# Peer layer, dense stage: its loads asked for in a fixed order four halves ahead, its gated rows sent from ScalarE's queue, its weight tables and maxima in small parts

## The chip, the core and the metric

The kernel runs on one core of a Trainium2 chip. The metric is the device time of one execution in microseconds (us). Each engine runs its own stream of instructions in the order in which the program holds them: TensorE (PE, with its weight loads as PEld), VectorE (DVE), ScalarE (ACT), GpSimd (POOL) and SyncE (SP). Transfers run on 16 DMA engines; SP, ACT and POOL ask for them, and an instruction that has to wait for something holds up whatever stands behind it in its stream.

## The reference

One transformer layer over 512 tokens of width 2048: an adaptive norm, a mixer (attention beside a recurrent unit), and a layer of 16,384 experts. Only the last matters here:

```
q = (h @ w_q) ...                       # two score vectors of 128 keys for each of 8 heads
v1, i1 = top_k(s1, 16); v2, i2 = top_k(s2, 16)
vs, ic = top_k(v1[..., :, None] + v2[..., None, :], 16)   # 16 of the 256 sums
e = i1[ic // 16] * 128 + i2[ic % 16]    # expert numbers: 128 per token
w = softmax(vs)
act = gelu(u[e] . h) * w                # 128 dot products per token
y = sum over the 128 of act * v[e]
```

`peer_u` and `peer_v` are 16,384 x 2048 in float32, 128 MB each.

## The kernel before, in words

Three of the four token groups of 128 (their numbers are 0, 2 and 3) are computed densely: all of `peer_u` is read once and multiplied with these 384 tokens. The fourth group, called side work here, fetches its 128 rows per token straight from `peer_u` and `peer_v`.

The dense stage runs over 128 blocks of 128 experts (`ublock`, L685), and each block over two halves of 1024 elements, so 256 halves. A half reads 512 KB into one of four `raw` buffers (`stream`, whose load is L99 on SP), rounds it on ACT into `shi` (L94), takes the rest on DVE into `slo` (L95), and PE multiplies: 8 pieces x 3 products (`shi` with `dh`, `shi` with `dl`, `slo` with `dh`), 24 matmuls of 384 columns (L690). `shi` and `slo` have three buffers each. After both halves ACT applies the gelu (L694) and SP writes the gated rows `ge` to two tables in HBM, 128 KB (L696) and 64 KB (L698).

`pump()` stands after every half. It sends on the side work at a rate of 0.9 (`side.send(GRATE)`): POOL asks for 128 rows, 1 MB, by an indirect DMA (L744) into one of four `gr` buffers, and two gathers later DVE uses it, for the dot products (L758, 128 times) or for the sum `y` (L756, 128 times). It also sends on one `scatter` (L886) when some are due.

Beside that, three more things run within the 128 blocks:

- `decode` (L624, L627, L628, operations on 128x2048 elements): from the top sixteen sums to expert numbers, once per token group. Group 0's stands before the first block, those of groups 2 and 3 before blocks 2 and 3, and the late group's after its own top-k (`tp0`, L588 to L604), whose scores SP reads back head by head (`s12`, L934, two buffers).
- `halves_of`: the weights of the chosen experts as a dense matrix. For each half-batch of 64 tokens 16 groups of four tokens: DVE makes one-hot tiles (L909, L914), PE multiplies them (L915), ACT copies the result into `ws` (L916). When the half-batch is done, SP writes `ws` to the tables in four parts of 1 MB (L920), in 256-byte pieces, and DVE takes four maxima `F` (L921). There are six half-batches.
- `make_list`: from the maxima to lists of the experts in use (L822, L823), with scatters on POOL.

A `pad` tile is set to zero on DVE (L811) and written to the first rows of the tables, and a `padi` to the lists (L812, L813, L817). It lies in memory that the decodes of groups 2 and 3 used before.

A scheduler simulates the engines and reorders each engine's stream by its own estimates. An instruction under `keep_in_program_order` stays behind the one that was written before it on its engine; only the gathers, the scatters and one step of the lists are so marked before.

After the dense stage the v stage (from about 2356 us) gathers the rows of `peer_v` that are in use, with their gates from the tables, and multiplies them; the rest of the side work's `y` runs beside it.

Of the kernel before, what the change touches and what calls it, by code (L numbers as in the profile page):

```python
# [9 lines left out]
F32 = mybir.dt.float32  # L10
F32R = mybir.dt.float32r
# [4 lines left out]
OP = mybir.AluOpType  # L16
AX = mybir.AxisListType
# [7 lines left out]
NB = 128  # L25
# [34 lines left out]
def program(ctx: ExitStack, tc: tile.TileContext, a):  # L60
    nc = tc.nc
    V, A, PE, G = nc.vector, nc.scalar, nc.tensor, nc.gpsimd
# [5 lines left out]
    raw = pool(ctx, "raw", 4)  # L68
    hl = pool(ctx, "hl", 3)
# [23 lines left out]
    def hilo(hi, lo, src):  # L93
        A.copy(hi, src)  # L94
        V.tensor_tensor(out=lo, in0=src, in1=hi, op=OP.subtract)  # L95

    def stream(src, n=1024):
        r = raw.tile([128, 1024], F32, name="raw")
        nc.sync.dma_start(r[:, :n], src)  # L99
        hi = hl.tile([128, 1024], F32R, name="shi")  # L100
        lo = hl.tile([128, 1024], F32R, name="slo")
        hilo(hi[:, :n], lo[:, :n], r[:, :n])
        return hi, lo
# [14 lines left out]
    tab1 = dram.tile([NROW + 128, 256], F32, name="tab1")  # L118
    tab2 = dram.tile([NROW + 128, 512], F32, name="tab2")
# [16 lines left out]
    for half in range(2):  # L136
        r = raw.tile([128, 1024], F32, name="raw")[:1]
# [31 lines left out]
    def pbank():  # L169
        return ps.tile([128, 512], F32, name="pj", tag="pj", bufs=2)  # L170

    for q in range(4):
        p = pbank()
# [7 lines left out]
    with tc.tile_pool(name="pro", bufs=1, reuse_waits="tile") as pro:  # L181
# [7 lines left out]
        for t in range(NT):  # L189
# [7 lines left out]
            r = rstd(pro, ss, 1, 1.0 / D)  # L197
            dg = pro.tile([128, 128], F32, name="dg", bufs=2)
            V.tensor_scalar(dg, ident, r, None, op0=OP.mult)
            for k4 in range(4):  # L200
                p = pbank()
# [62 lines left out]
    p = pbank()  # L264
# [9 lines left out]
    p = bank()  # L274
# [211 lines left out]
    for b0 in range(0, 8, 2):  # L486
# [6 lines left out]
        ge = [lru_y(b) for b in bs]  # L493
# [26 lines left out]
    for q in range(4):  # L520
# [8 lines left out]
        for k2 in range(KC // 2):  # L529
            w = stream(a["w_out"][q, k2])  # L530
# [8 lines left out]
        for t in range(NT):  # L539
# [4 lines left out]
            m = mp.tile([128, 512], F32, name="x1", tag="m")  # L544
# [5 lines left out]
            if q == 3:  # L550
                s4 = const.tile([128, 1], F32, name="s4", bufs=4)
                V.tensor_reduce(s4, ssq[:, t], axis=AX.X, op=OP.add)
                w = const.tile([128, 128], F32, name="dg", bufs=4)
# [6 lines left out]
    with tc.tile_pool(name="wk2", bufs=12, reuse_waits="tile") as wk2:  # L560
        for q in range(4):
            pr = bank()
            for k4 in range(4):
                k = q * 4 + k4
                p = bank()
# [80 lines left out]
    for h in range(H):  # L646
# [6 lines left out]
        for half in range(2):  # L653
            p = pbank()
# [10 lines left out]
            p = bank()  # L665
            c0 = half * 128
# [13 lines left out]
            G.tensor_copy(dl[k], wl2[k][:, 128:])  # L680
    hps.close()

    def ublock(b):
        p = pbank()
        for half in range(2):  # L685
            uh, ul = stream(a["peer_u"][b, half])
            for k8 in range(8):
                k = half * 8 + k8
                for i, (l, r) in enumerate(three(uh, ul, dh[k], dl[k])):
                    PE.matmul(p[:, :NDT], l[:, k8 * 128:k8 * 128 + 128], r, start=(k == 0 and i == 0),  # L690
                              stop=(k == KC - 1 and i == 2))
            pump()
        ge = gq.tile([128, NDT], F32, name="ge")
        A.activation(ge, p[:, :NDT], AF.Gelu_apprx_tanh)  # L694
        rows = slice(128 + b * 128, 256 + b * 128)
        nc.sync.dma_start(tab2[rows].rearrange("p (t x) -> p t x", t=2)[:, :, 0:128],  # L696
                          ge[:, 128:384].rearrange("p (t x) -> p t x", t=2))
        nc.sync.dma_start(tab1[rows, 0:128], ge[:, 0:128])  # L698

    dn = ExitStack()  # L700
    otp = pool(dn, "otp", side="right")
# [3 lines left out]
    todo = []  # L705
# [5 lines left out]
    def ublocks(upto):  # L711
        while blk[0] < upto:
            ublock(blk[0])
            blk[0] += 1
# [76 lines left out]
    def scatter_some(n):  # L791
        for _ in range(n):
            if scatters:
                scatters.pop(0)()

    todo.append(lambda: side.send(GRATE))
    todo.append(lambda: scatter_some(1))
    for t in (1, 2):
# [97 lines left out]
    TH = 64  # L896
    sets = {}

    def halves_of(dz, t, o, tab, c0, lo, step):
        Fs = []  # L900
        for hf in range(2):
            h0 = hf * TH
            ws = dz.tile([128, NB, TH], F32, name="ws")
            for t4 in range(TH // 4):
                ublocks(lo + hf * step + t4 * (step - 3) // (TH // 4))
                p = bank()
                o1 = dz.tile([128, 4, 128], F32, name="o1", bufs=2)
                t0 = h0 + t4 * 4
                V.tensor_tensor(out=o1, in0=iota[:, None, :].to_broadcast([128, 4, 128]),  # L909
                                in1=o[:, 0, t0:t0 + 4, None].to_broadcast([128, 4, 128]), op=OP.is_equal)  # L910
                for j in range(4):
                    tt = t0 + j
                    o2 = dz.tile([128, 128], F32, name="o2", bufs=6)
                    V.tensor_scalar(o2, iota, o[:, 1, tt:tt + 1], o[:, 2, tt:tt + 1], op0=OP.is_equal, op1=OP.mult)  # L914
                    PE.matmul(p[:, j * 128:j * 128 + 128], o2, o1[:, j], start=True, stop=True)  # L915
                A.copy(ws[:, :, t4 * 4:t4 * 4 + 4].rearrange("p i t -> p t i"), p.rearrange("p (t i) -> p t i", t=4))  # L916
            F = dz.tile([128, NB], F32, name="F", bufs=4)
            for i in range(4):
                sl = slice(i * 32, i * 32 + 32)
                nc.sync.dma_start(tab[128 + i * 4096:4224 + i * 4096, c0 + h0:c0 + h0 + TH].rearrange("(i p) t -> p i t", p=128), ws[:, sl])  # L920
                V.tensor_reduce(F[:, sl], ws[:, sl], axis=AX.X, op=OP.max)  # L921
            Fs.append(F)
        V.tensor_tensor(out=Fs[0], in0=Fs[0], in1=Fs[1], op=OP.max)
        return Fs[0]
# [191 lines left out]
    r = inv(1)  # L1116
# [75 lines left out]
```

## Time and profile before

| | us |
|---|---|
| median of 3 runs | 3125.18 (3118.3 to 3130.12) |
| the profiled execution | 3117.84 |
| its span | 3116.0 |
| dense stage (first L690 to the last) | about 1073 to 2356 |
| v stage and end | 2356 to 3116 |

The columns of the profile: a group of instructions is given by line, engine, operation and tiles with its count, its busy time, the mean of one in ns, and the idle time of the engine just ahead of it with what ended that. Over the whole span PE is busy 92%, DVE 80%, ACT 39% and POOL 30%, and the 16 DMA engines move 279 GB/s.

### The profile page before, as it was taken

The page shows a single profiled execution, that of the slowest core. Times are in us where ns is not written, and L with a number is a line of the kernel's source. Part 1 is how long each engine was busy: PE and PEld are TensorE (multiplying, and loading weights), DVE is VectorE, ACT ScalarE, POOL GpSimd, SP SyncE. Part 2 cuts the span into 40 slices and gives each one's busy share as a digit, 9 for nine tenths or more (in the row PEclk, how much of TensorE's full clock was granted, in tenths as well). Part 3 has the DMA queues.
Part 4 walks back from the last instruction along what each step waited for, and adds up shares of the span by engine and source line. Part 5 has one row for each costly group of instructions (what it writes and reads, how often), then busy time and mean ns, then how long its engine had stood idle before and what let it go on. Part 6 is the DMA issues. An engine that isn't in the chain of part 4 may idle for free.

```text
span 3116.0 us, 39002 instructions
## 1 busy us (share of the span) xinstructions
PE 2859.3 (92%) x14093; PEld 2497.1 (80%) x14093; DVE 2487.7 (80%) x4100; ACT 1221.3 (39%) x1653; POOL 928.6 (30%) x673
## 2 busy tenths in 40 slices
PE   7899999989999999988899989998878999888887
PEld 5577777768788899988889989998877777766665
DVE  6877777873368898999988889999768888777777
ACT  5322223662232243333322223334223444555665
POOL 0000000000020002222223352422448777477774
PEclk9999999999999999999999999999989999999999
DMA  9767777333322368999999989999989999978885
GB/s 344 292 226 232 246 234 237 111 106 129 122 89 90 109 203 331 334 320 304 313 394 402 400 307 345 347 297 307 343 336 397 371 353 359 350 278 321 344 317 218
DMA packets 329502, 869.30 MB, mean 279 GB/s; under 512 B 125682, under 2 KB 181362, under 8 KB 274388
## 3 DMA queue, kind: packets, MB, share of 16 engines
q0 software_dynamic: 72512, 477.03, 40.5%
q1 hardware_dynamic: 256352, 389.52, 37.3%
q8 instruction: 112, 1.84, 0.2%
q14 instruction: 90, 0.74, 0.1%
q10 hardware_dynamic: 436, 0.18, 0.0%
HBM read 805.38 MB, written 61.25 MB: 278 GB/s over the span
## 4 chain that ended last, share of the span: by engine, by line
PE 56%; DVE 12%; DMA 10%; issue 7%; ACT 3%; POOL 2%; SPq 1%; another core or an unknown queue 0%; DVEq 0%; ACTq 0%; POOLq 0%
PE pj L690 25%; PE ps L991 11%; PE pj L660 6%; PE ps L526 4%; DMA araw<-w_ada 4%; DVE slo L95 4%; PE pj L302 3%; PE pj L991 2%; PE ps L915 2%; DVE gr L758 1%; DMA raw<-tab,igown 1%; PE pj L526 1%; DVE F L921 1%; ACT shi L94 1%; POOL gr L744 1%
## 5 line engine op out<-in xcount | busy, mean ns | idle before, releaser
L690 PE MATMUL pj<-dh,slo 128*128 128x384 f32 x2048 | 698.9, 343 | 53.7 <-DVE slo L95 53.5
L690 PE MATMUL pj<-dh,shi 128*128 128x384 f32 x2048 | 699.6, 342 | 21.1 <-ACT shi L94 21.1
L690 PE MATMUL pj<-dl,shi 128*128 128x384 f32 x2048 | 696.8, 340 | 0.0
L94 ACT CAST shi<-raw 128x1024 fp32r<-128x1024 f32 (+1 forms) x402 | 417.6, 1047 | 632.8 <-PE pj L690 243.5
L95 DVE TENSOR_TENSOR slo<-raw,shi 128x1024 fp32r<-128x1024 f32 (+1 forms) x402 | 487.7, 1217 | 217.1 <-ACT shi L94 196.3
L690 PEld LDWEIGHTS pj<-dh,slo 128*128 128x128 f32 x2048 | 392.4, 192 | 60.8 <-DVE slo L95 60.4
L95 DVE TENSOR_TENSOR slo<-gr,shi 128x1024 fp32r<-128x1024 f32 x342 | 405.6, 1222 | 41.4 <-ACT shi L94 34.6
L690 PEld LDWEIGHTS pj<-dh,shi 128*128 128x128 f32 x2048 | 393.3, 192 | 22.2 <-ACT shi L94 22.2
L690 PEld LDWEIGHTS pj<-dl,shi 128*128 128x128 f32 x2048 | 392.5, 192 | 0.1
L94 ACT CAST shi<-gr 128x1024 fp32r<-128x1024 f32 x342 | 342.1, 1046 | 107.6 <-PE ps L991 60.2
L744 POOL DMA_INDIRECT gr<-u_rows,ei x128 | 173.9, 1358 | 678.5 <-DVE gr L758 313.9
L756 DVE SCALAR_TENSOR_TENSOR y<-gr,dots,y 128x2048 f32<-128x2048 f32 x128 | 300.7, 2349 | 36.7 <-DMA gr<-v_rows,ei 36.4
L991 PE MATMUL ps<-shi,gh 128*128 128x512 f32 x740 | 254.0, 414 | 73.3 <-ACT gh L94 42.0
L148 DVE SCALAR_TENSOR_TENSOR araw<-araw,sil 128x1024 f32<-128x1024 f32 x192 | 233.8, 1222 | 104.8 <-DMA araw<-w_ada 101.9
L991 PE MATMUL ps<-slo,gh 128*128 128x512 f32 x740 | 297.4, 408 | 6.9 <-DVE slo L95 6.9
L758 DVE SCALAR_TENSOR_TENSOR gr<-gr,hrow 128x2048 f32<-128x2048 f32 x128 | 292.3, 2284 | 4.0 <-issue 4.0
L744 POOL DMA_INDIRECT gr<-v_rows,ei x128 | 198.3, 1549 | 311.4 <-DVE y L756 161.3
L991 PE MATMUL ps<-shi,gl 128*128 128x512 f32 x740 | 275.2, 399 | 1.6 <-DVE gl L95 1.6
L679 POOL CAST dh<-hh 128x384 fp32r<-128x384 f32 x16 | 10.4, 648 | 855.1 <-DVE hh L573 855.1
L991 PEld LDWEIGHTS ps<-shi,gh 128*128 128x128 f32 x740 | 143.9, 196 | 122.2 <-ACT gh L94 50.3
L694 ACT ACTIVATE ge<-pj 128x384 f32<-128x384 f32 x128 | 62.8, 490 | 422.4 <-PE pj L690 334.5
L302 PE MATMUL pj<-hh,shi 128*128 128x512 f32 x528 | 214.0, 405 | 6.6 <-ACT w L478 3.5
(353 smaller groups left out, 4996.2 us busy)
## 6 DMA issues: line engine op xcount, KB each, us to landing
raw<-peer_u SPq DMA_DIRECT2D x256, 512.0 KB
araw<-w_ada SPq DMA_DIRECT2D x192, 512.0 KB
raw<-w_in SPq DMA_DIRECT2D x66, 512.0 KB
tab<-ws SPq DMA_DIRECT2D x24, 1024.0 KB
raw<-w_out SPq DMA_DIRECT2D x32, 512.0 KB
raw<-w_q SPq DMA_DIRECT2D x32, 512.0 KB
tab<-ge SPq DMA_DIRECT2D x128, 128.0 KB
tab<-ge SPq DMA_DIRECT2D x128, 64.0 KB
```

What stands on the lines that cost most here:

```text
L94: A.copy(hi, src)
L95: V.tensor_tensor(out=lo, in0=src, in1=hi, op=OP.subtract)
L148: V.scalar_tensor_tensor(out=r, in0=r, scalar=1.0, in1=sil[:, half * 1024:half * 1024 + 1024], op0=OP.mult, op1=OP.mult, accum_out=acc[:, ...
L302: PE.matmul(p, l[:, k8 * 128:k8 * 128 + 128], r, start=(k == 0 and i == 0), stop=(k == KC - 1 and i == 2))
L526: PE.matmul(po[t], l[:, ts], r[:, sl], start=(k == 0 and i == 0), stop=(k == KC - 1 and i == 2))
L660: PE.matmul(p, l[:, k8 * 128:k8 * 128 + 128], r, start=(k == 0 and i == 0), stop=(k == KC - 1 and i == 2))
L690: PE.matmul(p[:, :NDT], l[:, k8 * 128:k8 * 128 + 128], r, start=(k == 0 and i == 0), stop=(k == KC - 1 and i == 2))
L694: A.activation(ge, p[:, :NDT], AF.Gelu_apprx_tanh)
L744: return G.indirect_dma_start(out=out, out_offset=None, in_=src, in_offset=bass.IndirectOffsetOnAxis(ap=idx, axis=0))
L756: V.scalar_tensor_tensor(out=y0, in0=r, scalar=dots[:, j:j + 1], in1=y0, op0=OP.mult, op1=OP.add)
L758: V.scalar_tensor_tensor(out=r, in0=r, scalar=1.0, in1=hrow, op0=OP.mult, op1=OP.mult, accum_out=dots[:, j:j + 1])
L991: PE.matmul(banks[t][half * 2 + q2], l[:, ts], x[:, sl], start=first and i == 0, stop=end and i == 2)
```

## The change

Loads. The `peer_u` loads have a function of their own (`uload`). Before each half it asks for loads up to four halves ahead, and each load is kept in program order on SP: it stays behind the SP instruction that was written just before it, whichever that is.

Gated rows. The two `ge` writes of a block leave from ACT's queue.

Weights and maxima. A half-batch writes `ws` in 32 parts of 128 KB, each kept in program order on SP, and its four maxima stand between them as single entries of a list; `pump()` takes five entries of that list after every half. The token groups of a half-batch end two blocks sooner, and the blocks that are left of its share run after them.

```diff
+    loads = []
+    asked = [0]
+
+    def uload(upto):
+        while asked[0] < min(upto, 2 * NB):
+            r = raw.tile([128, 1024], F32, name="raw")
+            tc.keep_in_program_order(nc.sync.dma_start(r, a["peer_u"][asked[0] // 2, asked[0] % 2]))
+            loads.append(r)
+            asked[0] += 1
+
     def ublock(b):
         p = pbank()
         for half in range(2):
-            uh, ul = stream(a["peer_u"][b, half])
+            uload(2 * b + half + 4)
+            uh = hl.tile([128, 1024], F32R, name="shi")
+            ul = hl.tile([128, 1024], F32R, name="slo")
+            hilo(uh, ul, loads.pop(0))
...
-        nc.sync.dma_start(tab2[rows].rearrange("p (t x) -> p t x", t=2)[:, :, 0:128],
+        nc.scalar.dma_start(tab2[rows].rearrange("p (t x) -> p t x", t=2)[:, :, 0:128],
                           ge[:, 128:384].rearrange("p (t x) -> p t x", t=2))
-        nc.sync.dma_start(tab1[rows, 0:128], ge[:, 0:128])
+        nc.scalar.dma_start(tab1[rows, 0:128], ge[:, 0:128])
...
+    slices = []
+
+    def slices_some(n):
+        for _ in range(n):
+            if slices:
+                slices.pop(0)()
+
+    todo.append(lambda: slices_some(5))
     todo.append(lambda: side.send(GRATE))
     todo.append(lambda: scatter_some(1))
...
-                ublocks(lo + hf * step + t4 * (step - 3) // (TH // 4))
+                ublocks(lo + hf * step + t4 * (step - 5) // (TH // 4))
...
-            for i in range(4):
-                sl = slice(i * 32, i * 32 + 32)
-                nc.sync.dma_start(tab[128 + i * 4096:4224 + i * 4096, c0 + h0:c0 + h0 + TH].rearrange("(i p) t -> p i t", p=128), ws[:, sl])
-                V.tensor_reduce(F[:, sl], ws[:, sl], axis=AX.X, op=OP.max)
+
+            def write(i, ws=ws, c=c0 + h0):
+                tc.keep_in_program_order(nc.sync.dma_start(
+                    tab[128 + i * 512:640 + i * 512, c:c + TH].rearrange("(i p) t -> p i t", p=128), ws[:, i * 4:i * 4 + 4]))
+
+            def most(i, ws=ws, F=F):
+                V.tensor_reduce(F[:, i * 32:i * 32 + 32], ws[:, i * 32:i * 32 + 32], axis=AX.X, op=OP.max)
+
+            for i in range(32):
+                slices.append(lambda i=i, w=write: w(i))
+                if i % 8 == 4:
+                    slices.append(lambda i=i // 8, m=most: m(i))
+            ublocks(lo + hf * step + step)
             Fs.append(F)
```

Three places show how the streams differ. In the changed kernel the load is L689, the gather use for the dots L771, the one for `y` L769, the pad writes L833, L834 and L838, the one-hot tiles L930 and L935, the `s12` loads L964, the `ws` writes L941.

SP before, where the writes of `pad` and `padi` stand: 33 loads of `peer_u` have been asked for by then.

```order
L99 DMA raw<-peer_u 128x1024 x2
L696 DMA tab_87<-ge 256x1x128
L698 DMA tab_86<-ge 128x128
L99 DMA raw<-peer_u 128x1024
L812 DMA tab_87<-pad 128x512
L813 DMA tab_86<-pad 128x256
L817 DMA list_88<-padi 128x16
```

SP of the changed kernel at the same place; the first row is the load of the side group's token rows `hrow`:

```order
L735 DMA hrow<-hspill 128x2048
L689 DMA raw<-peer_u 128x1024 x4
L673 DMA sspill<-sc_8295 128x128
L689 DMA raw<-peer_u 128x1024 x5
L833 DMA tab_87<-pad 128x512
L834 DMA tab_86<-pad 128x256
L838 DMA list_88<-padi 128x16
L838 DMA list_89<-padi 128x20
L689 DMA raw<-peer_u 128x1024 x23
```

The pad writes now stand behind 9 loads instead of 33, and the first load stands behind `hrow`; before, six loads stand ahead of `hrow`.

SP where the late group's scores are read back for its top-k, the last four of eight such loads. Before:

```order
L934 DMA s_14913<-sspill 128x2x128
L696 DMA tab_87<-ge 256x1x128
L698 DMA tab_86<-ge 128x128
L890 DMA sg_14585<-list_88 128x16
L99 DMA raw<-peer_u 128x1024
L696 DMA tab_87<-ge 256x1x128
L698 DMA tab_86<-ge 128x128
L934 DMA s_14935<-sspill 128x2x128
L99 DMA raw<-peer_u 128x1024 x3
L934 DMA s_15034<-sspill 128x2x128
```

In the changed kernel:

```order
L964 DMA s_15040<-sspill 128x2x128
L689 DMA raw<-peer_u 128x1024
L964 DMA s_15062<-sspill 128x2x128
L689 DMA raw<-peer_u 128x1024 x2
L964 DMA s_15084<-sspill 128x2x128
L964 DMA s_15106<-sspill 128x2x128
L964 DMA s_15128<-sspill 128x2x128
L964 DMA s_15150<-sspill 128x2x128
L689 DMA raw<-peer_u 128x1024 x29
```

Loads of `peer_u` stood between these reads before; now the last four stand together, and all later loads behind them.

DVE in the decode of the late group, where the operations on 128x2048 (`eq`, `se`) and the sums `y` stand. Before:

```order
L624 TENSOR_TENSOR eq<-abf,iota 128x2048
L756 SCALAR_TENSOR_TENSOR y_8378<-gr,dots,y_8378 128x2048
L638 TENSOR_TENSOR wv<-wv,sm 128x128
L627 TENSOR_TENSOR eq<-eq,idf 128x2048
L95 TENSOR_TENSOR slo<-raw,shi 128x1024
L756 SCALAR_TENSOR_TENSOR y_8378<-gr,dots,y_8378 128x2048
L628 TENSOR_REDUCE se<-eq 128x128
L95 TENSOR_TENSOR slo<-raw,shi 128x1024
L756 SCALAR_TENSOR_TENSOR y_8378<-gr,dots,y_8378 128x2048
L624 TENSOR_TENSOR eq<-abf,iota 128x2048
L95 TENSOR_TENSOR slo<-raw,shi 128x1024
```

In the changed kernel:

```order
L624 TENSOR_TENSOR eq<-abf,iota 128x2048
L638 TENSOR_TENSOR wv<-wv,sm 128x128
L769 SCALAR_TENSOR_TENSOR y_8378<-gr,dots,y_8378 128x2048
L627 TENSOR_TENSOR eq<-eq,idf 128x2048
L769 SCALAR_TENSOR_TENSOR y_8378<-gr,dots,y_8378 128x2048
L628 TENSOR_REDUCE se<-eq 128x128
L769 SCALAR_TENSOR_TENSOR y_8378<-gr,dots,y_8378 128x2048
L624 TENSOR_TENSOR eq<-abf,iota 128x2048
L769 SCALAR_TENSOR_TENSOR y_8378<-gr,dots,y_8378 128x2048
L627 TENSOR_TENSOR eq<-eq,idf 128x2048
L769 SCALAR_TENSOR_TENSOR y_8378<-gr,dots,y_8378 128x2048
```

The `slo` rows that stood between the decode's steps are gone from this place; the next one stands after all of the decode. All in all the changed DVE stream has three long stretches in the dense stage without a `slo`: between those of halves 8 and 9 (9 uses for the dots, 14 decode operations on 128x2048, 17 L935, 4 L930 and the `pad` memset), between 150 and 151 (9 `y` and 49 small operations of the top-k), and between 156 and 157 (19 `y`, 6 decode operations, 12 L935, 3 L930). By the end of the stage 229 uses of gathers stand in the DVE stream, 210 before.

## Rows read from the trace of the kernel before

**Rows 1.** Windows of core 0: length, busy time, granted clock, DMA share, rate

```profile
core 0: us, PE busy (x) PEld busy (x) DVE busy (x) ACT busy (x) POOL busy (x), PEclk, DMA share, GB/s
1073.00:2356.00 1283.00, 1197.63 (x6945) 1186.42 (x6944) 1144.56 (x1620) 421.84 (x498) 390.43 (x266) 0.96 0.93 328
...
1303.00:1320.00 17.00, 15.97 (x97) 15.46 (x96) 17.00 (x18) 3.88 (x5) 1.88 (x2) 1.00 1.15 310
1570.00:1780.00 210.00, 210.00 (x1206) 210.00 (x1206) 171.35 (x152) 61.23 (x76) 68.07 (x51) 0.99 1.02 404
2356.00:2660.00 304.00, 284.73 (x1200) 224.84 (x1199) 253.95 (x273) 137.29 (x180) 229.31 (x154) 0.98 0.96 373
```

**Rows 2.** Groups of PE by line, dense stage, 1073 to 2356 us

```profile
L690 PE MATMUL pj<-dh,shi 128*128 128x384 f32 x2048 | 699.6, 342 | 21.1 <-ACT shi L94 21.1
L690 PE MATMUL pj<-dh,slo 128*128 128x384 f32 x2048 | 698.9, 343 | 53.7 <-DVE slo L95 53.5
...
L915 PE MATMUL ps<-o,o 128*128 128x128 f32 x768 | 115.8, 288 | 10.6 <-ACT ws L916 4.2 <-DVE o L909 3.9 <-DVE o L914 2.0
```

**Rows 3.** Timeline of PE: the idle time ahead of one matmul in brackets

```profile
1568.43 0.69 PE L690 MATMUL pj<-dh,shi 128*128 128x384 f32 x1 [7.25 <-ACT shi L94]
...
2195.71 0.69 PE L690 MATMUL pj<-dh,shi 128*128 128x384 f32 x1 [7.56 <-ACT shi L94]
...
2291.54 0.69 PE L690 MATMUL pj<-dh,slo 128*128 128x384 f32 x1 [13.20 <-DVE slo L95]
```

**Rows 4.** Timeline of SP's queue, 1532 to 1565 us: start, length of the issue

```profile
1532.95 24.49 SPq L920 DMA_DIRECT2D tab<-ws  x4
1557.53 5.92 SPq L99 DMA_DIRECT2D raw<-peer_u  x1
1563.55 0.53 SPq L696 DMA_DIRECT2D tab<-ge  x1
1564.13 0.60 SPq L698 DMA_DIRECT2D tab<-ge  x1
```

**Rows 5.** Chain of waits, 1530 to 1580 us: start, length, what

```profile
1557.53 9.73 DMA raw<-peer_u
```

**Rows 6.** Groups of DVE by line, dense stage, 1073 to 2356 us

```profile
L95 DVE TENSOR_TENSOR slo<-raw,shi 128x1024 fp32r<-128x1024 f32 x254 | 308.8, 1221 | 73.5 <-ACT shi L94 53.6 <-ACT ge L694 18.4 <-issue 1.2
L758 DVE SCALAR_TENSOR_TENSOR gr<-gr,hrow 128x2048 f32<-128x2048 f32 x128 | 292.3, 2284 | 4.0 <-issue 4.0
L756 DVE SCALAR_TENSOR_TENSOR y<-gr,dots,y 128x2048 f32<-128x2048 f32 x93 | 218.5, 2350 | 35.1 <-DMA gr<-v_rows,ei 34.8
L914 DVE TENSOR_SCALAR o<-iota,oT 128x128 f32<-128x128 f32 x384 | 116.5, 346 | 16.3 <-PE ps L915 15.8
L909 DVE TENSOR_TENSOR o<-iota,oT 128x512 f32<-128x512 f32 x96 | 65.6, 683 | 0.7 <-PE ps L915 0.4
L921 DVE TENSOR_REDUCE F<-ws 128x32 f32<-128x2048 f32 x24 | 53.2, 2277 | 1.3 <-issue 1.3
...
L624 DVE TENSOR_TENSOR eq<-abf,iota 128x2048 f32<-128x2048 f32 x8 | 18.3, 2288 | 0.1
...
L592 DVE MAX8 v<-mr 128x8 f32<-128x128 f32 x22 | 5.9, 284 | 0.0
```

**Rows 7.** Timeline of DVE, 1256 to 1261 us: start, length

```profile
1256.72 1.21 DVE L95 TENSOR_TENSOR slo<-raw,shi 128x1024 fp32r<-128x1024 f32 x1
1257.85 2.28 DVE L758 SCALAR_TENSOR_TENSOR gr<-gr,hrow 128x2048 f32<-128x2048 f32 x1
...
1260.06 0.61 DVE L914 TENSOR_SCALAR o<-iota,oT 128x128 f32<-128x128 f32 x2
```

**Rows 8.** Timeline of SP's queue at the stage's start

```profile
1071.26 0.38 SPq L722 DMA_DIRECT2D hrow<-hspill  x1
```

**Rows 9.** Timeline of PE at the stage's start

```profile
1072.87 0.34 PE L690 MATMUL pj<-dh,shi 128*128 128x384 f32 x1
```

**Rows 10.** Timeline of DVE at the memset of `pad`

```profile
1186.71 0.48 DVE L811 MEMSET pad<- 128x512 f32 x1
```

## The prediction

> **What bounds the kernel now.** I read the windows first, because the change touches one stage only. From 1073 to 2356 us PE is busy 1197.6 of 1283 us, DVE 1144.6, and the DMA engines show a share of 0.93 [rows 1]. Three resources stand close together, so the question is which one is late at each place. In the fed stretch, 1570 to 1780 us, PE never rests: 1206 matmuls in 210 us, 0.174 us from one to the next, so a half (24 matmuls) costs 4.18 us, while DVE is busy 171 of 210 [rows 1]. That is what the stage looks like when PE is the bound.
>
> Next come PE's groups by line, for what it waits for elsewhere: 53.7 us ahead of the matmuls that need `slo`, 21.1 ahead of those that need `shi`, 10.6 ahead of L915, together 85.4 us [rows 2]. The reader should then open the long waits one by one. Two of them, 7.25 and 7.56 us, have ACT's cast named [rows 3], but the first stands behind a load: SP spends 24.49 us on asking for the four `ws` writes, and asks for the next load only at 1557.53 [rows 4]; the chain then runs for 9.73 us through that load [rows 5]. The longest, 13.20 us at 2291.54 [rows 3], has DVE named; in that stretch DVE itself waits for gathers, which is part of the 34.8 us under L756 [rows 6].
>
> Last, DVE's groups. It waits 73.5 us ahead of its `slo`, mostly for ACT's casts [rows 6]. DVE keeps its program order: if no `slo` stands in it for some time, PE can work only on what it has in hand, and three `shi`/`slo` buffers mean under three halves, 12.5 us.
>
> **What the change costs: three stretches without a slo.** The loads are now kept behind whatever SP instruction was written before them. The pad writes stand behind 9 loads, and need a memset that comes after the decodes, at 1186.71 before [rows 10], 114 us into the stage; four `s12` reads, which need the top-k to advance, now stand in one row ahead of a load. So DVE's stream has the rest of the decode and of the top-k, with gather uses, and no `slo` between. I price these stretches by DVE's steps from start to start: a gather use for the dots 1260.06 - 1257.85 = 2.21 us, `slo` 1257.85 - 1256.72 = 1.13 [rows 7]. Each is some 0.07 to 0.09 below its mean, so I take that off the others too: `y` 2.27, a decode operation 2.21, L909 0.60, L914 0.27, a small top-k operation 0.2 to 0.35 [rows 6].
>
> - After half 8: 9 x 2.21 + 14 x 2.21 + 17 x 0.27 + 4 x 0.60 = 57.8, and 6.7 for the memset and some twenty small operations: 64.5 us. PE may enter it with the full lead, 2.75 halves or 11.5 us: it waits 53.
> - After half 150: 9 x 2.27 + 49 small ones at about 0.32 = 36.0. PE comes with less than a half in hand, as two shorter gaps stand ahead: it waits 33.
> - After half 156: 19 x 2.27 + 6 x 2.21 + 12 x 0.27 + 3 x 0.60 = 61.4, with the small ones 67.7. Less 7.7 in hand: it waits 60.
>
> Sum 146 us. These operations are not new; they came out of other places, where less is now late. I walked both DVE streams with these steps and the rule that `slo` h needs the matmuls of h - 3 done and the matmuls of h need `slo` h. For before the walk gives 72 us of PE waits, for the changed stream 162, of which 16 lie outside the three stretches. In the late part, halves 184 to 224, DVE has only 86 us of work against 167 of PE: the slack is there, but too late to be used. So this term is 162 - 72 = **+90**. Bounds: the trace has 85.4 - 7.25 - 7.56 - 13.2 - 2.6 (a wait like the last, just ahead of it) = 55 where the walk has 72, so it errs by 17 or more, and PE's lead into a stretch can be off by a half or two: +60. If the 28 `y` in the two late stretches wait for their gathers, 1 MB each at 328 GB/s [rows 1] or 3.2 us against 2.27, that is up to 26 more: some +110.
>
> **The start.** Six loads stood ahead of `hrow`; now none does. The first L690 began at 1072.87 [rows 9], `hrow` was asked for at 1071.26 [rows 8]. With a load's wait of 9.73 us [rows 5] the first matmul could be 9.7 late; if `hrow` itself moves up with the loads, 0. I take half, as the DMA engines are quieter there than at 1557: **+4.5**.
>
> **What goes.** The bunch of four `ws` issues (24.49 us of SP) becomes 32 small ones between the loads, and loads are asked for four halves ahead: the two `shi` waits, 14.8 us, should go, and the late 13.2 + 2.6, which hang on gathers behind the list's scatters, should go too, as the scatters move up: **-31**, bounds 0 and -31, since I can name no more. The four maxima in a row (4 x 2.2) no longer delay a `slo` by 9 us; that is inside the walk.
>
> **What comes with the drains.** A half-batch now leaves within 8 halves: 8 loads 4.2 MB, 7.2 gathers 7.5, `ws` 4.2, `ge` 0.8, 16.7 MB in all. At 404 GB/s (the fed stretch) that is 41 us, at 310 (a stretch full of small pieces, DMA share 1.15) 54 [rows 1], against 8 x 4.18 = 33.4 of PE. Four loads asked for ahead cover up to 16.7 us. So each drain ends between 0 and 4 us late if the lead is full, and about 10 if it is half gone: six drains, 0 to +60. I take 2 each, **+12**, as the DVE stretches leave the DMA engines time to catch up.
>
> **ge on ACT.** 128 x (0.53 + 0.60) = 145 us of issuing [rows 4] moves to an engine that is busy 422 of 1283 us [rows 1]: nothing, hidden by ACT's idle time. If ACT's issue waits for a transfer, the next `shi` stands behind it; that belongs to the drains' upper bound. The Trainium skill, page "DMA: Bandwidth & Descriptors", section "Issuing engines are not separate DMA queues", says that transfers asked for by different engines end on the same 16 DMA engines and that only the sequencer's issue time is saved; the same page's "Rules for kernel authors" wants 1 MiB or more per transfer. Both speak against this change, and the 128 KB parts go the other way. The trace has the `ws` writes at 256 bytes a piece whatever their number, so I see no size effect here; by the page the drains would be at their upper end.
>
> **The v stage.** 229 - 210 = 19 `y` leave it. Its DMA share to 2660 is 0.96 but PE idles just 304 - 284.7 = 19 us there [rows 1], and most of the 19 `y` were beside PE's work: **-12**, bounds 0 and -19.
>
> **Sum.** 90 + 4.5 - 31 + 12 - 12 = +63.5 on the profiled execution's 3117.84: 3181.3. The median stands 7.3 above that execution, so 3188.7 on its scale; I say 3188. Own range: the low ends (60 + 0 - 31 + 0 - 19) give +10, the high ends (110 + 9.7 + 0 + 60 + 0) +180; they won't all fall on one side, and I take +25 to +105, 3150 to 3230.
>
> **Rivals.**
>
> The transfers are the true bound (faster). The DMA share is 0.93 over the whole stage [rows 1], and PE's waits for `slo` could themselves stem from late casts (53.6 us of DVE's idle time ahead of `slo` hangs on `shi` [rows 6]). Then loads asked for early, spread writes and 20 MB of gathers taken out of the v stage decide: 90 + 4.5 against 72 us of waits returned in the dense stage and 20 MB / 373 GB/s = 54 us in the v stage [rows 1]: -31.5, 3086 in the profile, **3094**. It decides from about 110 us returned. Against it: the fed stretch runs at a share of 1.02 and PE never waits; and the v stage shows only 19 us to give back. Half as strong it ends near zero.
>
> The order doesn't cost what I think (same): if PE keeps more in hand, or the stretches coincide with waits of before, the first term falls to 30: +3, **3128**. For it: the walk's error of 17. Against it: DVE keeps its order, and there are only three buffers.
>
> The drains become the bound (slower still): `ws`, gathers and loads together at 310 GB/s, 10 us late each, +60, nothing of the 31 returned: 90 + 4.5 + 60 - 12 = +142, **3267**. For it: ACT now issues in between, and the casts stand behind it. Against it: 404 GB/s was moved with PE fed.
>
> **How the numbers follow.** Forecast 0.69, drains 0.13, transfers as true bound 0.09, order cheaper 0.09. Half a percent, 15.6 us, is about what a measurement here tells from no change: 3109.6 to 3140.8. The forecast's own low end still counts as slower; slower is 0.69 + 0.13 less a little for its tail, 0.80; same 0.11; faster 0.09. The range leaves out the faster case and the upper part of the drains: 3122 to 3245.
>
> **What would show it.** Three PE waits of some 53, 33 and 60 us, all ended by DVE's `slo`: the first at about 1115 to 1165, the others near halves 150 and 156; in each the DVE busy with decode, top-k and gather uses. The `pad` memset at about 1165. No PE wait of 7 us behind a load after a `ws` write. PE without waits in halves 184 to 224. 101 uses for `y` before the stage ends. The forecast is wrong if the dense stage is shorter than 1283 us, if one of the three waits is under 20 us, or if the longest waits hang on `shi` or on loads.

## The result, and the profile after

The changed kernel takes 3266.3 us (median of 6 runs, 3256.8 to 3279.1) beside 3121.7 for the kernel before in the same comparison: a ratio of 1.0476, 95% interval 1.0453 to 1.0499. It is slower, as forecast, but by 145 us where 63 were forecast, and it lies outside the range, which ended at 3245.

The profiled execution has a span of 3257.1 us, 141.1 more than before. The stage from the first dense matmul to the last grew from 1283.0 to 1439.2 us (+156.2), it began 2.9 us later, and what follows it became 18.0 us shorter (760.1 to 742.1). So the whole loss is in the stage that the change touches. First its windows: the stage, then the three stretches that the prediction named, then the rest of the kernel. The columns are those of [rows 1].

```profile
core 0: us, PE busy (x) PEld busy (x) DVE busy (x) ACT busy (x) POOL busy (x), PEclk, DMA share, GB/s
1075.00:2515.00 1440.00, 1217.48 (x6931) 1194.88 (x6932) 1170.50 (x1628) 427.89 (x499) 404.81 (x277) 0.91 0.85 301
1117.00:1176.00 59.00, 7.99 (x33) 5.54 (x31) 49.54 (x56) 5.52 (x7) 10.79 (x11) 0.56 0.51 198
1937.00:1962.00 25.00, 1.94 (x11) 1.62 (x10) 25.00 (x73) 1.21 (x2) 7.17 (x7) 0.62 0.90 317
1992.00:2049.00 57.00, 5.52 (x24) 4.28 (x23) 57.00 (x55) 3.62 (x5) 32.49 (x17) 0.55 0.82 303
2515.00:3257.00 742.00, 660.53 (x2692) 515.30 (x2690) 572.98 (x761) 403.01 (x552) 482.81 (x358) 0.96 0.86 324
```

The reader is to see two things in the three middle rows: VectorE is busy in all of them (49.5 of 59 us, 25 of 25, 57 of 57), and TensorE does almost nothing. In the first row the granted clock is 0.91 where the stage before had 0.96 [rows 1], and PE needs 1217.5 us of busy time where it needed 1197.6, for nearly the same number of matmuls. The matmuls after a stop run at a lower clock, as after the second one:

```profile
1966.80:1969.80 3.00, 2.92 (x9) 2.92 (x10) 3.00 (x3) 0.00 (x0) 0.00 (x0) 0.50 1.00 411
1972.00:1980.00 8.00, 8.00 (x48) 8.00 (x47) 8.00 (x16) 2.49 (x3) 1.42 (x2) 1.00 0.99 341
```

After 23 us in which PE stood still, 9 matmuls take 3 us at a granted clock of 0.50 (the lower level, 1.2 GHz); a little later 48 take 8 us at 1.00 (2.4 GHz).

PE's groups by line in the stage, the counterpart of [rows 2]:

```profile
L703 PE MATMUL pj<-dh,shi 128*128 128x384 f32 x2048 | 707.1, 345 | 67.9 <-ACT shi L94 67.6
L703 PE MATMUL pj<-dh,slo 128*128 128x384 f32 x2048 | 705.4, 345 | 43.7 <-DVE slo L95 43.4
...
L936 PE MATMUL ps<-o,o 128*128 128x128 f32 x768 | 112.2, 289 | 27.1 <-DVE o L935 23.1 <-DVE o L930 3.9
L745 PE MATMUL ps<-ident,se 128*128 128x128 f32 x6 | 2.8, 461 | 84.7 <-DVE se L631 41.4 <-DVE se L628 36.5 <-DVE sm L637 6.9
```

The transposes of the fourth row read so in the kernel before:

```profile
L732 PE MATMUL ps<-ident,se 128*128 128x128 f32 x6 | 1.6, 272 | 0.0
```

Together PE waits 223.5 us in this window, of which 221.8 lie behind the first dense matmul; before it was 85.4, counted from there too. The new wait is that of L745, the transposes at the end of a decode: 84.7 us for six matmuls that waited 0 before. They stand in PE's stream ahead of the next half's matmuls, so PE stops at them rather than at a `slo`. The other growth is `shi`, 21.1 to 67.9 us. Of that, 23.1 us are one wait in the second stretch, told of below; where the rest comes from is in ACT's waits, by what was waited for, total, times, longest:

```profile
ACT shi L94 <- DMA tab<-ws: 81.1, 9, 16.2
...
ACT ge L707 <- DMA tab<-ge: 46.7, 9, 7.1
...
ACT shi L94 <- DMA raw<-peer_u: 25.6, 11, 10.8
```

ACT's cast doesn't use `ws`. It is late because a gated-row write stands ahead of it in ACT's queue and waits there; of several such waits the row names the one that ended last. The timelines of ACT and, in the last row, of SP show one such place:

```profile
1473.64 0.49 ACT L707 ACTIVATE ge<-pj 128x384 f32<-128x384 f32 x1 [1.34 <-DMA raw<-peer_u]
1486.39 0.59 ACTq L709 DMA_DIRECT2D tab<-ge  x1
1487.14 0.54 ACTq L711 DMA_DIRECT2D tab<-ge  x1
1487.78 1.04 ACT L94 CAST shi<-raw 128x1024 fp32r<-128x1024 f32 x1 [13.65 <-DMA tab<-ws]
...
1475.58 0.51 SPq L689 DMA_DIRECT2D raw<-peer_u  x1
```

`ge` is finished at 1474.1; its first write is asked for only at 1486.39, and the cast behind it starts 13.65 us late. By the instructions in the trace every transfer of SP and ACT here uses one of eight completion counters, which the two queues share, and an issue waits until the transfer that had its counter last has landed. The first write's counter was that of the load which SP asked for at 1475.58, between parts of `ws`; it landed at 1486.32. The second write's was that of a `ws` part, which landed at 1487.12, and this is the one that the row names. Adding up the PE waits that overlap with such a wait of ACT gives 31.7 us. Going by the counters instead gives 29.5: 23 behind `ws` parts and 6 behind loads.

### The profile page after: what moved, and what is told of

Same layout as the page of the kernel before. It is cut to its first block, busy times and chain, and to the rows that moved or that the text cites. A ratio compares the mean times of both kernels' runs of the same rounds, so it can differ in the third digit from the quotient of the medians.

```text
span 3257.1 us, 39079 instructions
## 1 busy us (share of the span) xinstructions
PE 2879.8 (88%) x14093; PEld 2507.2 (77%) x14093; DVE 2489.1 (76%) x4100; ACT 1224.6 (38%) x1652; POOL 908.4 (28%) x673
## 4 chain that ended last, share of the span: by engine, by line
PE 47%; DVE 18%; DMA 15%; issue 14%; ACT 4%; POOL 2%; SPq 1%; ACTq 0%; DVEq 0%; POOLq 0%
PE pj L703 15%; PE ps L1021 11%; DMA araw<-w_ada 7%; PE pj L660 5%; DVE slo L95 4%; PE ps L526 4%; PE pj L302 2%; DVE gr L771 2%; PE pj L1021 2%; DMA tab<-ws 2%; PE ps L220 2%; DMA tab<-ge 2%; DVE araw L148 2%; DVE y L769 2%; ACT shi L94 1%
## 5 line engine op out<-in xcount | busy, mean ns | idle before, releaser
L703 PE MATMUL pj<-dh,shi 128*128 128x384 f32 x2048 | 707.1, 345 | 67.9 <-ACT shi L94 67.6
L703 PE MATMUL pj<-dh,slo 128*128 128x384 f32 x2048 | 705.4, 345 | 43.7 <-DVE slo L95 43.4
L757 POOL DMA_INDIRECT gr<-u_rows,ei x128 | 204.5, 1598 | 648.0 <-DVE gr L771 302.4
L769 DVE SCALAR_TENSOR_TENSOR y<-gr,dots,y 128x2048 f32<-128x2048 f32 x128 | 300.2, 2346 | 27.9 <-DMA gr<-v_rows,ei 27.7
L771 DVE SCALAR_TENSOR_TENSOR gr<-gr,hrow 128x2048 f32<-128x2048 f32 x128 | 291.2, 2283 | 13.2 <-DMA gr<-u_rows,ei 13.1
L757 POOL DMA_INDIRECT gr<-v_rows,ei x128 | 177.4, 1386 | 278.6 <-DVE y L769 143.7
L302 PE MATMUL pj<-hlo,shi 128*128 128x512 f32 x528 | 213.4, 404 | 0.0
```

Of the source, the lines that this page charges most:

```text
L302: PE.matmul(p, l[:, k8 * 128:k8 * 128 + 128], r, start=(k == 0 and i == 0), stop=(k == KC - 1 and i == 2))
L757: return G.indirect_dma_start(out=out, out_offset=None, in_=src, in_offset=bass.IndirectOffsetOnAxis(ap=idx, axis=0))
L769: V.scalar_tensor_tensor(out=y0, in0=r, scalar=dots[:, j:j + 1], in1=y0, op0=OP.mult, op1=OP.add)
L771: V.scalar_tensor_tensor(out=r, in0=r, scalar=1.0, in1=hrow, op0=OP.mult, op1=OP.mult, accum_out=dots[:, j:j + 1])
```

## The experiments

The change has three parts: the pinned loads (P), the gated rows on ACT's queue (G), and the weights in 32 parts with the maxima between them (W). The first runs take them apart.

**Loads held behind each other only.** The loads keep their order among themselves, and nothing else of the change is touched.

```diff
-            tc.keep_in_program_order(nc.sync.dma_start(r, a["peer_u"][...]))
+            with tc.issue_after(last.pop().ins):      # behind the load before
+                d = nc.sync.dma_start(r, a["peer_u"][...])
+            last.append(d)
```

> The changed kernel, but each load is held behind the load before it only, not behind whatever SP instruction was written before it; gated rows still leave from ScalarE's queue and the weights in 32 parts. Theory of the order: the pinning behind the pad writes, the ws parts and the s12 reads is what took the slo out of three stretches of VectorE's stream; with it go some 130 us of PE waits and part of the 18 us of lower clock: 3266 - 130 to - 150, about 3115 to 3140. Theory of ScalarE's queue (its casts stand behind ge writes that wait for a ws part): nothing much changes, above 3230. Theory of the transfers (more small writes and earlier gathers load the DMA engines): nothing much changes either, above 3220.

(The first load, which has none before it, is free.) Measured: 3190.7 us, ratio 1.0224 (1.0179 to 1.0269), outside every range that was expected. The three stretches are gone: the longest time in VectorE's trace from one `slo` to the next is 28.9 us, where the changed kernel has 73.3, 66.0 and 34.7. Some 75 us came back, not 130 to 150: in the stage PE waits 142.5 us where the changed kernel had 223.5, and it is more than the kernel before has. ACT's casts still wait for `ws` parts, 60.0 us in 8 waits:

```profile
ACT ge L713 <- DMA tab<-ws: 64.6, 3, 25.8
ACT shi L94 <- DMA tab<-ws: 60.0, 8, 16.6
```

**Gated rows back on SP**, loads pinned and weights in parts as in the changed kernel.

```diff
-        nc.scalar.dma_start(tab2[rows]..., ge[:, 128:384]...)
-        nc.scalar.dma_start(tab1[rows, 0:128], ge[:, 0:128])
+        nc.sync.dma_start(tab2[rows]..., ge[:, 128:384]...)
+        nc.sync.dma_start(tab1[rows, 0:128], ge[:, 0:128])
```

> The changed kernel with the two gated-row writes of a block back on SP; loads pinned and weights in parts as in the changed kernel. Theory of the order: the three stretches stay, only the 32 us of PE waits that stand behind ACT's wait for ws parts go, and some of the clock: 3266 - 30 to - 45, about 3220 to 3236. Theory of ScalarE's queue: most of the loss goes, about 3130 to 3160. Theory of the transfers: unchanged within 0.5%, 3250 to 3282, as the same bytes move.

Measured: 3383.1 us, ratio 1.0827 (1.0790 to 1.0865). All theories missed: by the medians it is 117 us slower than the changed kernel, by the ratios some 110. SP's waits, by what was waited for, say why:

```profile
SPq L709 <- ACT ge L707: 812.4, 100, 69.0
```

A pinned load stands behind the gated-row write that was written before it, and that write waits for the gelu, thus for PE to finish the block. The lead of four halves shrinks to what PE leaves. With the writes on ACT's queue this wait leaves SP. So G is a remedy for P, and costs something only where the loads aren't pinned.

**Both edits**: loads behind each other, gated rows on SP; W is left alone.

> Both of the two edits: loads held behind the load before only, gated rows on SP. What is left of the change are the 32 parts with the maxima between them and the earlier end of the token groups. Theory of the order: 3085 to 3125, the four bunched writes of 24 us being gone. Theory of the transfers: the small parts alone cost, above 3160. If the two effects add up, it lies below the run with the load edit alone by the amount that the ge edit alone gives.

Measured: 3175.3 us, ratio 1.0172 (1.0139 to 1.0204). The parts by themselves cost some 50 us, where the first theory had them as a gain; the theory of the transfers, above 3160, has the time right. The two edits don't add up: putting the gated rows back on SP gives some 15 us here, hardly clear of the intervals, and took 117 with the loads pinned.

**The pins alone**, put into the kernel before (`uload` as in the change; `ge` on SP, `ws` in four writes).

> The kernel before with one part of the change alone: loads asked for four halves ahead and pinned behind the SP instruction written before them; ge writes on SP and ws writes in four of 1 MB, as before. Theory of the order: its VectorE stream has a stretch of 63 us without a slo after half 8 and seven of 15 to 20 us later: 3122 + 70 to + 130, 3190 to 3250. Theories of ScalarE's queue and of the transfers: neither is touched here, 3105 to 3140.

Measured: 3298.6 us, ratio 1.0555 (1.0517 to 1.0592), more than the whole change, and beyond the range expected. SP's waits again:

```profile
SPq L709 <- ACT ge L707: 814.8, 113, 28.5
...
SPq L825 <- DVE padi L828: 41.8, 1, 41.8
```

Both come from pinning a load behind something that isn't a load.

**Three loads freed.** In the program as written the SP entry just ahead of the loads of halves 9 and 157 is the marker that opens a memory pool, `dz` and `dz2`; such a marker has to wait for the decodes whose memory the pool reuses. Ahead of load 151 it is the eighth `s12` read. These three loads alone were held behind the load before instead:

```diff
+            if asked[0] in (9, 151, 157):
+                with tc.issue_after(last.ins):
+                    last = nc.sync.dma_start(r, a["peer_u"][...])
+            else:
+                last = tc.keep_in_program_order(nc.sync.dma_start(r, a["peer_u"][...]))
```

> The changed kernel with three of its 256 loads freed: the loads of halves 9, 151 and 157, which the changed kernel pins behind the opening of a memory pool (9 and 157) or behind the eighth s12 read (151), are held behind the load before them only; the other loads stay pinned, ge on ACT. Theory A, these three pins cost the 130 us of PE waits: they go, 3266 - 100 to - 150, 3115 to 3165. Theory B, a pinned load is a barrier wherever work that stands before it in the program has been put off, and the order just puts it off to the next pin: the stream of this kernel has its long stretches without slo now ahead of halves 32 (91 us of VectorE work) and 180 (96 us), so about the same PE waits at other places: 3235 to 3290, with two PE waits of 60 to 85 us in all at each of these halves and none over 5 us before half 30.

Measured: 3257.1 us, ratio 1.0468 (1.0448 to 1.0488): no gain clear of the intervals, as theory B has it. PE waits 3.3 us in all before half 30. What moved shows in the windows of halves 30 to 36 and 176 to 184:

```profile
1210.00:1327.00 117.00, 67.94 (x303) 59.16 (x302) 106.87 (x158) 20.95 (x23) 38.81 (x28) 0.65 0.95 316
2043.00:2177.00 134.00, 74.67 (x350) 67.27 (x348) 127.60 (x162) 30.38 (x33) 44.33 (x28) 0.69 0.82 278
```

Six halves take 117 us and eight take 134, where the changed kernel needed 43.4 and 45.5 between the same halves. That is some 160 us more there; at the three old places (halves 8 to 11, 148 to 152, 155 to 159) it is 156 less. The form of the loss was missed: the single waits are small (19.4 us the longest), PE waits 49 and 59 us in these two windows, and the rest is matmuls at a clock of 0.65 and 0.69 and the one-hot products crowded between them. How the rest divides between these two was not measured.

**Gated rows alone**, put into the kernel before.

> The kernel before with one part of the change alone: the two gated-row writes of a block leave from ACT's queue; loads free, ws in four writes of 1 MB. VectorE's order is nearly that of before. Theory that ACT's queue is a burden by itself (its casts stand behind a ge write that waits for a ws write of 1 MB): 10 to 40 us slower than before, 3136 to 3166, with ACT's casts waiting for tab<-ws at the six bunches. Theory that the issues are hidden: within 0.5% of before, 3110 to 3142. If SP, which waits 390 us for ge before, asks earlier for its loads then: up to 20 us faster.

Measured: 3133.9 us, ratio 1.0059 (1.0041 to 1.0078): 18 to 21 us. That is the loss of the first theory, but the interval doesn't shut out the second, which allowed 0.5%; and the mark of the loss shows at the `ws` copies (34.9 us of ACT's idle time, on `tab<-ws`) more than at the casts. SP asked earlier for nothing that mattered: it then waits for buffers instead (233.4 us in the same row before).

```profile
SPq L99 <- DVE slo L95: 672.4, 169, 12.7
```

**All parts at once**: as the run with both edits, with the list emptied after one half, so that the 32 parts stand in a bunch.

```diff
-    todo.append(lambda: slices_some(5))
+    todo.append(lambda: slices_some(40))
```

> As the run with both edits (loads behind the load before only, gated rows on SP, 3175), but the list of ws parts and maxima is emptied at once after the half at which a half-batch ends, so the 32 parts stand in a bunch as the four writes did before. Theory that the number of parts costs (32 issues took 32.3 us of SP in one bunch there, four took 24.5 before): 6 bunches x 8 us and what hangs on the single ws buffer, 3160 to 3190, no better than 3175. Theory that the spreading costs (the ws buffer is free later, the next half-batch's copies wait): back to 3115 to 3145.

Measured: 3190.7 us, ratio 1.0249 (1.0231 to 1.0267). The first bunch on SP's queue:

```profile
1303.97 30.12 SPq L947 DMA_DIRECT2D tab<-ws  x32
1338.15 1.80 SPq L692 DMA_DIRECT2D raw<-peer_u  x3
```

In the kernel before:

```profile
1302.24 17.63 SPq L920 DMA_DIRECT2D tab<-ws  x4
1319.97 7.29 SPq L99 DMA_DIRECT2D raw<-peer_u  x1
```

The bunch of 32 takes longer, but part of the difference lies with the load behind the four, which is itself held. Over the stage SP spends 202 us on asking for `ws` here and 113 before; with the loads it is 303 and 251. PE waits up to 27.6 us for a cast behind a load (at 1803). So taking the parts in a bunch doesn't give W's cost back; what the number of parts has to do with it the next run shows.

**Four large writes, spread**: as the run with both edits, but four entries of 1 MB, each followed by its maximum, one taken per half.

```diff
-                    tab[128 + i * 512:640 + i * 512, ...]..., ws[:, i * 4:i * 4 + 4]))
+                    tab[128 + i * 4096:4224 + i * 4096, ...]..., ws[:, i * 32:i * 32 + 32]))
...
-            for i in range(32):
+            for i in range(4):
                 slices.append(lambda i=i, w=write: w(i))
-                if i % 8 == 4:
-                    slices.append(lambda i=i // 8, m=most: m(i))
+                slices.append(lambda i=i, m=most: m(i))
...
-    todo.append(lambda: slices_some(5))
+    todo.append(lambda: slices_some(1))
```

> As the run with both edits (3175), but ws leaves in four writes of 1 MB, which stand in the list with the four maxima, one entry taken after each half, so a half-batch leaves over 8 halves in few large writes. Theory that the number of parts costs: 3115 to 3145, near before. Theory that the spreading costs: 3165 to 3190.

Measured: 3140.8 us, ratio 1.0087 (1.0065 to 1.0109). By the ratios, 1.0172 and 1.0087, half of what W costs is gone with the number of parts, some 27 of 54 us; about 0.9% is left.

**Pins and gated rows without the parts**: the changed kernel with `halves_of` as before. It fills the last place of the table below.

> The changed kernel with the weights as before: pinned loads and gated rows on ACT's queue, but ws in four writes of 1 MB and the maxima behind them. It closes the table of the three parts: the pins alone gave 3299, pins with parts 3383, pins with parts and ge on ACT 3266. If the parts cost the same here as without pins (3175 - 3122 = 53): 3266 - 53 = 3213. If the parts only cost where SP bunches them, and pins spread them between the loads: about 3266. If VectorE's long stretches set the time (its stream has 65.6 us after half 8 and 26 after 156 where the changed kernel has 65.6, 36 and 67): 3266 - 75 = 3190.

Measured: 3187.4 us, ratio 1.0255 (1.0220 to 1.0291), as the third of its expectations had it. PE's waits at the three places are 53.0, 0.2 and 15.7 us, 69 against 136 in the changed kernel; the first is the same.

**Fewer writes in the kernel before**, two of 2 MB and one of 4 MB per half-batch. The second edit:

```diff
+            nc.sync.dma_start(tab[128:128 + NROW, c0 + h0:c0 + h0 + TH].rearrange("(i p) t -> p i t", p=128), ws)
             for i in range(4):
                 sl = slice(i * 32, i * 32 + 32)
-                nc.sync.dma_start(tab[128 + i * 4096:4224 + i * 4096, ...]..., ws[:, sl])
```

> The kernel before with ws in two writes of 2 MB per half-batch in place of four of 1 MB, nothing else. Theory that the number of writes costs SP time and holds up its loads (four take 24.5 us, 32 took 32.3): at most 6 x 1 to 6 x 5 us shorter, 3095 to 3120 where before is 3120. Theory that the bytes and the 256-byte pieces set the length of a bunch: within 0.5% of before. Rival: a larger write keeps the ws buffer and the DMA queues longer, and the next half-batch or a load waits: 0.5 to 1% slower.

> The kernel before with ws in one write of 4 MB per half-batch. As the run with two writes, further along the same line: by the theory of the number of writes a little faster than with two; by that of the bytes the same as before; by the rival slower than with two, up to 2%.

Measured: 3109.9 us, ratio 1.0000 (0.9984 to 1.0015), and 3106.3, ratio 0.9986 (0.9969 to 1.0002). Nothing that can be told from the kernel before. With one write the first bunch reads:

```profile
1295.57 0.39 SPq L918 DMA_DIRECT2D tab<-ws  x1
1296.05 20.95 SPq L99 DMA_DIRECT2D raw<-peer_u  x1
```

The write itself is asked for in 0.39 us, but the load behind it takes 20.95, though by the trace its buffer had been free since 1294.33. With the load behind them, 4 MB hold SP for 21.4 us as one write and for 25.0 as four; the 32 parts above took 30.1 by themselves. The bytes are the same in all three, and so are the 256-byte pieces, so these rows can't say which of the two sets the hold; the number adds a few us.

**The end of the token groups alone**, put into the kernel before (`step - 5`, and `ublocks(lo + hf * step + step)` after the writes).

> The kernel before with one part of the change alone: the token groups of a half-batch end two blocks sooner (step - 5 in place of step - 3) and the blocks left of its share run after the ws writes; loads free, ge on SP, four writes of 1 MB and four maxima at once. The run with four spread writes (3141, 0.9% slower than before) holds this edit too. If this edit is what costs there: 0.6 to 1.2% slower than before, 3130 to 3150. If the spread is: within 0.4% of before.

Measured: 3113.4 us, ratio 0.9982 (0.9964 to 1.0000). It isn't what costs in the run with four spread writes.

Beside the kernel before, by parts:

| | W not | W |
|---|---|---|
| neither P nor G | 1 | 1.0172 |
| G | 1.0059 | 1.0224 |
| P | 1.0555 | 1.0827 |
| P and G | 1.0255 | 1.0476 |

(W without P was run with the loads held behind each other, which gives the kernel before the stream that it has.) By the ratios of these ratios (each ratio is known to some 0.2 to 0.45%) W costs 1.6 to 1.7% without P and 2.2 to 2.6% with it. P costs 1.9 to 2.5% beside G and 5.6 to 6.4% without. G costs 0.5 to 0.6% without P, which beside W is not clear of the intervals, and gives 2.9 to 3.3% with it. No version here beats the kernel before by more than its interval.

## Why the prediction was right or wrong

The direction was right, and so was the largest term; the size was not.

- **The three stretches, right in place and nearly in size.** 53, 33 and 60 us of PE waits were forecast, 146 in all; from half 8 to 11, 148 to 152 and 155 to 159 the trace has 52.4, 30.9 and 52.8, 136. The way of getting there was only half right. PE stood at the decodes' transposes in two of them, not at a `slo`, as the timeline of PE shows in one of them (in brackets the idle time ahead, as in [rows 3]); the second place is the one that hung on a cast:

```profile
1140.74 0.47 PE L745 MATMUL ps<-ident,se 128*128 128x128 f32 x1 [13.81 <-DVE se L631]
...
1961.73 0.69 PE L703 MATMUL pj<-dh,shi 128*128 128x384 f32 x1 [23.06 <-ACT shi L94]
```

None of the three longest waits (27.4, 23.1 and 20.2 us) was ended by DVE's `slo`, which the prediction had named as its sign. And in two of the three places it was not VectorE's order alone: the load itself was asked for late. SP's waits and its timeline:

```profile
SPq L833 <- DVE padi L836: 60.1, 1, 60.1
...
1929.29 24.23 SPq L964 DMA_DIRECT2D s<-sspill  x3
1953.56 104.58 SPq L689 DMA_DIRECT2D raw<-peer_u  x13
```

In the first SP stood 60.1 us at the writes of `pad`, and asked for the load of half 9 at 1159.60, though its buffer had been free since 1096.13. In the second the `s12` reads held the load of half 151 until 1953.56, 39 us after its buffer was free; the cast that PE waited for stands behind that load. In the third the loads had landed, that of half 157 some 67 us before its cast, and only the order of the streams was in the way.

Still it wasn't the pad writes or the `s12` reads as such: with three pins freed the loss moved to the next ones. What the runs show is that work which stands before a pinned load in the program and has been put off has to be done in a lump before that load, wherever the next pin is. The pins' part of the result, 1.0476 against 1.0224 or 75 us, is near the +90 of the term.
- **"What goes" and the credit of the walk, wrong; this is the step that failed.** The walk had the waits outside the stretches fall from 72 to 16 us, -31 was added for the waits behind loads, and +12 for the drains: -75 in all. Outside the stretches PE waits 85.7 us in the changed kernel (221.8 - 136.1), 85.4 before: nothing returned. The two `shi` waits are replaced by others: PE waits of some 8 us still stand after `ws` writes (at 1663 and 1689, for instance), now behind ACT's held gated-row writes. And the 32 parts are dearer than the four writes they replace: by the run with the parts as the only edit left W is some +53 us, not -19 (-31 + 12), about half of it by the number of parts. The drains term was +12 with an upper bound of 60; its upper bound was the better figure.
- **ge on ACT, costed at nothing, wrong both ways.** 31.7 us of PE waits stand behind it in the changed kernel, and by itself it costs 0.6%. The mechanism was named ("the next `shi` stands behind it") and put into the drains' bound, not into the sum. That without it the pinned loads would be much worse, by 110 to 117 us, was not seen at all. The Trainium skill's page "DMA: Bandwidth & Descriptors", section "Issuing engines are not separate DMA queues", states that issuing from several engines saves the sequencer's issue time only; here the gain of a second issuing queue was larger than that, since what it saved is a wait of SP ahead of its loads (812 us in the run without it).
- **The clock, left out.** PE's busy time in the stage grew by 20 us (1197.6 to 1217.5), at a granted clock of 0.91 against 0.96. The rows after the second stop, 0.50 and then 1.00, show how it comes; the sum has no term for it.
- **The start, right**: 2.9 us late, +4.5 forecast. **The v stage, right**: 18.0 us shorter, 12 forecast.
- **A slip that changes nothing**: 90 + 26 is 116, not 110, so the upper bound of the first term, and with it the sum of the high ends, is 6 us short.

Put together on the profiled executions: stretches 136 instead of 146 (-10), the rest of PE's waits 0 instead of -75 (+75), clock +20, start and v stage -8; 63.5 - 10 + 75 + 20 - 8 = 140.5, where 141.1 was measured.

**The rivals.** "The drains become the bound" had 3267 and met the number, by luck in part. Its mechanism accounts for part: ACT's casts behind its own queue are 32 us, and loads late in the drains show in the runs with W. But it counted 90 for the stretches where the pins give 75, had no clock, and missed that about half of W's cost goes with the number of its parts. That the order costs less (3128) is out: PE waits 136 us in the stretches. The transfers as the true bound are out: the DMA share of the stage fell from 0.93 to 0.85 and the time rose.

**What stays open.** With four large spread writes 0.9% remains (PE's waits are 107 us in its stage, 22 more than before), and neither the number of writes nor the end of the token groups explains it. The four writes are still kept in program order there and still spread over the halves; neither was taken away alone, so pins on the writes stay a rival. Why the parts cost 2.2 to 2.6% with pins, where SP doesn't bunch them, was not taken apart further.

## What to carry to other kernels

Holding an instruction "in program order" holds it behind whatever was written just before it on its engine, be it a pool's opening or a write that waits for the end of the block; hold it behind its own predecessor in the stream that is meant. In the order of the engine that is late, look for long stretches without the work that feeds the bound, and price them: that gave 146 us here and 136 were measured. Look also at what the pin itself waits for: here SP stood 60 us at a write ahead of a load whose buffer was free. A credit for waits that an edit is to remove wants a row that shows what will be in their place; where there is none, it belongs into the range and not into the sum.

## What was not expected of the hardware

The first bunch of 4 MB of `ws` held SP's queue for 17.6 us as four writes and 30.1 as 32 parts; as one write it took 0.39 us itself, and the load behind it was held for 20.95 us, with its buffer free. So the length of an issue in SP's row can belong to what was asked for before it, and not to the instruction. And where PE stopped and went, its granted clock was 0.55 to 0.69, and 0.50 just after a stop of 23 us. A stop costs more than its length: in the stage 136 us more of waits came with 20 us more of busy time for nearly the same matmuls (6931 records, 6945 before).
